# Moving the scan's second copies to ScalarE and the modulations' weight splits to VectorE, in a hybrid diffusion trunk

## The chip, the cores and the metric

The kernel runs on one core of a Trainium2 chip. In this kernel TensorE multiplies matrices, VectorE and ScalarE do most of the elementwise work and fetch the results of matmuls from PSUM, GpSimd does elementwise work between tiles in SBUF, and SyncE issues the transfers. Each engine has a queue of its own. The metric is the device time of one execution in microseconds; lower is better. The median of three runs is what a change is compared with, and the profile is of one execution more.

## The reference: what is computed

One inference step of a two-layer trunk over 128 context tokens and 512 latent tokens, with 1024 channels. Each layer is a normalisation, a modulation by shift, scale and gate, one input projection for three mixers, the mixers, and an output projection:

```
shift, scale, gate = split(silu(cond) @ w_mod[l] + b_mod[l], 3)
h = rmsnorm(x, norm_w[l]) * (1 + scale) + shift
a, b, c, gates = split(h @ w_in[l])
y = sigmoid(ga) * (attention_a(a) @ w_oa) + sigmoid(gb) * (attention_b(b) @ w_ob) + sigmoid(gc) * (scan_c(c) @ w_oc)
x = x + gate * (y @ w_out)
```

The third mixer is a scan over tokens, forward and backward, for 8 heads with a state of 64 x 64 each:

```
sa = state @ a_t
state = state * w_t + outer(sa, b_t) + outer(v_t, k_t)
y_t = state @ r_t
```

## The kernel before

**Numbers in two parts.** The weights come as float32. For every projection the kernel makes two tiles of each weight tile: `whi`, a rounded copy (ScalarE, line 176), and `wlo`, the rest (a subtraction, line 177), and the product is three matmuls instead of one (lines 227 to 229 for the projections). `load_split` does this for two halves of each 128-column block in the stage in question: transfer, cast, subtraction. Which engine subtracts is the argument `sub`: VectorE in most places, GpSimd for the weights inside attention and, before the change, for the modulations' weights.

**The modulations.** `modulation` computes 128 values of shift, scale or gate for both kinds of tokens: it loads and splits a block of `w_mod`, makes 16 matmuls of 4 columns (lines 249 and 250), copies a row and turns it by one more matmul. Layer 0 runs its 8 gate blocks and all 16 shift and scale blocks of layer 1 in this way between other work, layer 1 its own 8 gate blocks. That is 32 calls of two pieces each. They are called from `fillers` and, at the end, from `period`.

**The scan.** It is cut into chunks of 64 tokens: two for the context, eight for the latent tokens, in both directions at once, for four pairs of heads and two layers, which makes 80 steps. `c_scan` does a step as a chain through several engines:

- line 771: matmuls with the keys and the state give `sca` in PSUM;
- lines 773 and 774: two copies of 64 x 128 values bring it to `Wb` in SBUF, one for each head of the pair. Both read the same PSUM bank, and the framework lets the second engine read it only after the first one has ended;
- line 777: matmuls of `Wb` with the inverse matrices give `scb`;
- lines 779 and 780: two such copies bring it to `VZ`, again from one bank;
- line 782: GpSimd copies it to `Ub`; line 786: matmuls for the next state; line 790: matmuls that add to `sca`;
- lines 801 and 803: VectorE makes the next state, which line 771 of the next step reads; line 808: ScalarE copies the output.

**What runs beside it.** While the scan of one pair goes on, `pump` plays a stream of other work between its steps: input projections, gates, the modulations, and the preparation of the next pair. The last is `c_prep`, `c_pairs` and `c_inverse`. The inverse is a loop of 30 steps of two small VectorE instructions each (lines 662 and 664), between a transposition at line 656 and one at line 674, after which TensorE goes on with matmuls of 32 x 32 at line 683. There are eight of these inverses, four in each layer; the first of each layer runs before a scan.

**The order.** The program's order gives the dependences. The framework's scheduler then lays out each engine's queue with its own estimate of durations (`schedule_with_timeline_sim=True`, line 1624), so that instructions of the stream stand between those of one step. Weight tiles have two buffers of each kind (`NW = 2`), and the raw weights two.

Of the kernel before, what the change touches and what calls it, by code (L numbers as in the profile page):

```python
# [107 lines left out]
class Trunk:  # L108
# [595 lines left out]
    def c_scan(self, l, e, ps, rate, prev):  # L704

        nc, V, S, G, PE = self.nc, self.V, self.S, self.G, self.PE
        sm = cs = self.cs
        p, L1, AB, BT, gm, VZ = e.p, e.L1, e.AB, e.BK, e.gm, e.VZ

        def pc(name):  # L710
            return ps.tile([128, 512], F32, tag="c", name=name)

        PR = (slice(0, 64), slice(64, 128))
        QR = (slice(64, 128), slice(0, 64))

        e.YY = YY = cs.tile([128, 20, 64], F32, tag="YY", name="YY")
        step = 0
        for n, base in ((2, 0), (8, 2)):
            ctxp = n == 2
            if ctxp:  # L720
                for h in range(2):
                    G.memset(VZ[h][PR[h], 0:2, :], 0.0)
                Zg = sm.tile([128, 2, 64], F32, tag="Zg", name="Zg", bufs=2)
                G.memset(Zg, 0.0)
            else:
                Z0 = sm.tile([128, 2, 64], F32, tag="Z0", name="Z0")
                nc.sync.dma_start(out=Z0, in_=self.I["zinit"][l, p])
                for h in range(2):
                    r_ = PR[h]
                    S.copy(out=VZ[h][r_, base, :], in_=Z0[r_, 0])  # L730
                    S.mul(out=VZ[h][r_, base + n - 1, :], in_=Z0[r_, 1], mul=gm[r_, 10 + base + n - 1:10 + base + n])

            def pair(cf, cb):

                a, b = base + cf, base + cb
                if a < b:
                    return slice(a, b + 1, b - a)
                return slice(a, b - 1 if b else None, b - a)

            for k in range(n):  # L740
                cf, cb = k, n - 1 - k
                up = pair(cf, cb)
                uu = (base + cf, 10 + base + cb)
                cc = (base + cf, base + cb)
                last = k == n - 1
                need_z = ctxp or not last
                gi = (base + k, None if last else 10 + base + n - 2 - k)
                if need_z and not (ctxp and k == 0):
                    Zg = sm.tile([128, 2, 64], F32, tag="Zg", name="Zg", bufs=2)
                    for h in range(2):  # L750
                        r_ = PR[h]
                        if not last:
                            g2 = gm[r_, gi[0]:gi[1] + 1:gi[1] - gi[0]]
                            G.tensor_tensor(out=Zg[r_], in0=VZ[h][r_, up, :], in1=g2.unsqueeze(2).to_broadcast([64, 2, 64]),
                                            op=ALU.mult)
                        else:
                            G.tensor_scalar(out=Zg[r_, 0], in0=VZ[h][r_, cc[0], :], scalar1=gm[r_, gi[0]:gi[0] + 1],
                                            scalar2=None, op0=ALU.mult)
                            G.tensor_copy(out=Zg[r_, 1], in_=VZ[h][r_, cc[1], :])
                Wb, Ub = self.wbd[step % 2], self.ubd[step % 2]  # L760
                step += 1
                if step == 5 and prev:
                    self.c_out(prev, ps)
                ca, cb_ = pc("sca"), pc("scb")

                a4 = ca[:, 0:256].rearrange("p (d h i) -> p d h i", d=2, h=2)
                b4 = cb_.rearrange("p (x d h i) -> p x d h i", x=2, d=2, h=2)

                for h in range(2):
                    for d in range(2):  # L770
                        PE.matmul(a4[:, d, h], lhsT=L1[h][:, uu[d]].rearrange("p a s -> p (a s)"), rhs=VZ[h][:, cc[d], :],  # L771
                                  start=(h == 0 and d == 0), stop=False, skip_group_check=True)
                S.copy(out=Wb[PR[0], :, 0], in_=a4[0:64, :, 0])
                V.tensor_copy(out=Wb[PR[1], :, 1], in_=a4[0:64, :, 1])
                self.pump(rate)
                for d in range(2):
                    PE.matmul(cb_[:, d * 128:d * 128 + 128], lhsT=AB[:, uu[d]].rearrange("p a s -> p (a s)"),
                              rhs=Wb[:, d].rearrange("p h i -> p (h i)"), start=True, stop=True, skip_group_check=True)
                S.copy(out=VZ[0][PR[0], up, :], in_=b4[0:64, 0, :, 0])  # L779
                V.tensor_copy(out=VZ[1][PR[1], up, :], in_=b4[0:64, 0, :, 1])  # L780
                for h in range(2):
                    G.tensor_copy(out=Ub[PR[h], :, h], in_=VZ[h][PR[h], up, :])  # L782
                self.pump(rate)
                if need_z:
                    for d in range(2):
                        PE.matmul(cb_[:, 256 + d * 128:384 + d * 128], lhsT=BT[:, uu[d]].rearrange("p h i -> p (h i)"),  # L786
                                  rhs=e.VZt[:, :, cc[d], :], start=True, stop=True, skip_group_check=True)
                self.pump(rate)
                for d in range(2):
                    PE.matmul(ca[:, d * 128:d * 128 + 128], lhsT=AB[:, uu[d]].rearrange("p a s -> p (a s)"),  # L790
                              rhs=Ub[:, d].rearrange("p h i -> p (h i)"), start=False, stop=True, skip_group_check=True)
                if need_z:
                    if last:
                        Zf = sm.tile([128, 2, 64], F32, tag="Zf", name="Zf")
                    for h in range(2):
                        r_ = PR[h]
                        for d in range(2):
                            src = b4[r_, 1, d, h]
                            dst = Zf[r_, d] if last else VZ[h][r_, cc[d] + (1 if d == 0 else -1), :]
                            if gi[d] is None:  # L800
                                V.tensor_tensor(out=dst, in0=src, in1=Zg[r_, d], op=ALU.add)
                            else:
                                V.scalar_tensor_tensor(out=dst, in0=src, scalar=gm[r_, gi[d]:gi[d] + 1], in1=Zg[r_, d],  # L803
                                                       op0=ALU.mult, op1=ALU.add)
                    if last:
                        nc.sync.dma_start(out=self.O["nst"][l, p], in_=Zf)
                for h in range(2):
                    S.copy(out=YY[QR[h], uu[0]:uu[1] + 1:uu[1] - uu[0], :], in_=a4[64:128, :, h])
# [547 lines left out]
    def run(self):  # L1356
# [26 lines left out]
        def pool(ctx, name, bufs, **k):  # L1383
            return ctx.enter_context(tc.tile_pool(name=name, bufs=bufs, reuse_waits="tile", **k))

        self.early = set()
        ps = P("psA0", **PSA)
        with ExitStack() as ctx:
            wp = pool(ctx, "wp0", 1, side="right")
# [19 lines left out]
        for l in range(DEPTH):  # L1409
            plan = self.plan = NS(**PLAN[l])  # L1410
            if l:
                ps = P(f"psA{l}", **PSA)
            with ExitStack() as ctx, ExitStack() as ctx_c, ExitStack() as ctx_e:
                wp = pool(ctx, f"wp1{l}", 1)
# [14 lines left out]
                mods = [(l, ct) for ct in range(2 * KT, 3 * KT)]  # L1429
# [4 lines left out]
                def fillers(n):  # L1434
                    for _ in range(n):
                        yield from units.pop(0)
                        count[0] += 1
                        while mods and count[0] >= every:
                            count[0] -= every
                            yield from self.modulation(*mods.pop(0), wp, ps, self.G)  # L1440

                def keys(p):

# [54 lines left out]
                ps = P(f"psB{l}", f=1, pt=2, po=1, S=2)  # L1498
# [3 lines left out]
            ps = P(f"psC{l}", f=8)  # L1502
            with ExitStack() as ctx:
                wp = pool(ctx, f"wp3{l}", 1)
# [137 lines left out]
```

## Time and profile before

| | |
|---|---|
| median of three runs | 2282.05 us (2279.15 to 2290.32) |
| the profiled execution | 2288.99 us |
| its span, first to last instruction | 2287.3 us |
| TensorE busy | 2112.1 us (92%), 15380 matmuls |
| VectorE busy | 1547.8 us (68%), 3096 instructions |
| ScalarE busy | 1155.0 us (50%), 2574 instructions |
| GpSimd busy | 528.7 us (23%), 680 instructions |
| mean granted clock of TensorE | 0.947 of full speed |

The profile lists for each group of instructions the line, the engine, the operation, what it writes and reads, the count, the busy time with the mean of one in ns, and the idle time of the engine just before them with what ended it. PE is TensorE, DVE VectorE, ACT ScalarE, POOL GpSimd, SP SyncE. A wait is put down to the instruction whose semaphore came last.

### The profile page before, as it was taken

How to read it: one execution, taken by the hardware profiler on the slowest of the kernel's cores; microseconds unless marked ns; L12 is line 12 of the kernel's file. 1: busy time of each engine (PE TensorE's matmuls, PEld its weight loads, DVE VectorE, ACT ScalarE, POOL GpSimd, SP SyncE). 2: the span in 40 equal slices, each digit the busy share in tenths (PEclk: the TensorE clock that was granted, in tenths of full speed). 3: DMA queues.
4: the chain of work that ended last, by engine and by line, in shares of the span. 5: the costliest groups of instructions: out<-in, count | busy, mean ns of one | idle time of the engine just before them, and what ended most of it. 6: DMA issues, size and time to landing. Idle time of an engine off the chain costs nothing.

```text
span 2287.3 us, 40446 instructions
## 1 busy us (share of the span) xinstructions
PE 2112.1 (92%) x15380; PEld 2004.8 (88%) x15380; DVE 1547.8 (68%) x3096; ACT 1155.0 (50%) x2574; POOL 528.7 (23%) x680
## 2 busy tenths in 40 slices
PE   8989999999889889999989999998997888899998
PEld 6989999999788768889989999998997876788998
DVE  4666776877845677766647867668576467777673
ACT  4544545554444567762355545545353456677332
POOL 3121324234232221102031022221222222111111
PEclk9998989989899999999999999898897889999999
DMA  6232223222223311036612322232122221111562
GB/s 231 79 96 74 85 78 101 70 89 92 91 87 110 106 38 39 31 101 209 192 53 89 98 75 79 77 101 71 54 94 79 83 88 44 35 47 44 181 194 83
DMA packets 111763, 209.71 MB, mean 92 GB/s; under 512 B 14416, under 2 KB 33488, under 8 KB 111568
## 3 DMA queue, kind: packets, MB, share of 16 engines
q1 hardware_dynamic: 111568, 207.12, 28.3%
q8 instruction: 121, 1.98, 0.4%
q14 instruction: 74, 0.61, 0.1%
HBM read 163.52 MB, written 43.55 MB: 91 GB/s over the span
## 4 chain that ended last, share of the span: by engine, by line
PE 69%; DVE 15%; ACT 8%; issue 4%; DMA 3%; POOL 1%; DVEq 0%; SPq 0%; ACTq 0%; POOLq 0%
PE pcm L227 11%; PE pcm L228 10%; PE pcm L229 10%; PE sc L958 3%; PE pA L612 3%; PE sca L771 2%; PE pm L180 2%; PE pm L182 2%; PE pm L181 2%; PE pp L976 2%; PE scb L786 2%; DVE wlo L177 1%; PE pout L180 1%; PE pout L182 1%; PE pout L181 1%
## 5 line engine op out<-in xcount | busy, mean ns | idle before, releaser
L227 PE MATMUL pcm<-hh,whi 128*128 128x320 f32 x1952 | 630.9, 323 | 21.4 <-DVE modc L254 5.8
L229 PE MATMUL pcm<-hh,wlo 128*128 128x320 f32 x1952 | 621.4, 319 | 7.1 <-DVE wlo L177 7.1
L228 PE MATMUL pcm<-hl,whi 128*128 128x320 f32 x1952 | 620.8, 318 | 0.0
L227 PEld LDWEIGHTS pcm<-hh,whi 128*128 128x128 f32 x1952 | 377.3, 193 | 29.3 <-DVE modc L254 6.8
L229 PEld LDWEIGHTS pcm<-hh,wlo 128*128 128x128 f32 x1952 | 376.3, 193 | 10.4 <-DVE wlo L177 9.4
L228 PEld LDWEIGHTS pcm<-hl,whi 128*128 128x128 f32 x1952 | 377.4, 193 | 1.3
L176 ACT CAST whi<-wraw 128x512 fp32r<-128x512 f32 (+1 forms) x356 | 226.3, 666 | 295.8 <-PE pcm L228 104.1
L177 DVE TENSOR_TENSOR wlo<-wraw,whi 128x512 fp32r<-128x512 f32 (+1 forms) x262 | 208.1, 809 | 84.9 <-ACT whi L176 83.5
L177 POOL TENSOR_TENSOR wlo<-wraw,whi 128x512 fp32r<-128x512 f32 x94 | 123.4, 1328 | 161.4 <-ACT whi L176 126.2
L782 POOL COPY ubd<-VZ 64x128 f32<-64x128 f32 x160 | 62.4, 390 | 406.2 <-ACT VZ L779 345.1
L961 DVE TENSOR_REDUCE nm<-sc 128x1 f32<-128x640 f32 x128 | 104.4, 819 | 27.7 <-PE sc L958 26.3
L166 DVE TENSOR_TENSOR pl<-pp,ph 128x512 fp32r<-128x512 f32 x160 | 107.0, 684 | 22.5 <-ACT ph L165 19.6
L182 PE MATMUL pm<-yh,wlo 128*128 128x320 f32 x384 | 118.9, 310 | 0.3 <-DVE wlo L177 0.3
L180 PE MATMUL pm<-yh,whi 128*128 128x320 f32 x384 | 118.8, 309 | 0.0
L181 PE MATMUL pm<-yl,whi 128*128 128x320 f32 x384 | 118.6, 309 | 0.0
L963 ACT ACTIVATE P<-sc,nm 128x640 f32<-128x640 f32 x128 | 102.0, 798 | 26.7 <-DVE nm L961 22.0
L165 ACT CAST ph<-pp 128x512 fp32r<-128x512 f32 x160 | 91.7, 588 | 37.8 <-PE pp L976 20.3
L976 PE MATMUL pp<-small,P 128*128 128x128 f32 x640 | 98.4, 278 | 2.7 <-ACT RB L1004 2.2
L771 PE MATMUL sca<-VZ,L 128*128 128x64 f32 x640 | 94.6, 286 | 3.0 <-DVE VZ L803 2.2
L771 PEld LDWEIGHTS sca<-VZ,L 128*128 128x128 f32 x640 | 91.2, 208 | 6.0 <-DVE VZ L803 4.0
L976 PEld LDWEIGHTS pp<-small,P 128*128 128x128 f32 x640 | 78.1, 143 | 12.8 <-ACT RB L1004 4.3
L662 DVE TENSOR_TENSOR NF<-LN 128x30 f32<-128x30 f32 (+14 forms) x240 | 84.9, 354 | 6.5
(376 smaller groups left out, 4800.1 us busy)
## 6 DMA issues: line engine op xcount, KB each, us to landing
wraw<-in_win SPq DMA_DIRECT2D x156, 256.0 KB, 3.0
wraw<-in_wg SPq DMA_DIRECT2D x96, 256.0 KB, 3.1
wraw<-in_wmod SPq DMA_DIRECT2D x64, 256.0 KB, 3.0
gsp<-gt SPq DMA_DIRECT2D x48, 320.0 KB, 2.5
gt<-gsp SPq DMA_DIRECT2D x48, 320.0 KB, 3.3
wraw<-in_wo SPq DMA_DIRECT2D x24, 512.0 KB, 4.3
cm<-gsl SPq DMA_DIRECT2D x26, 320.0 KB, 2.6
wraw<-in_wmod SPq DMA_DIRECT2D x16, 512.0 KB, 6.8
```

What stands on the lines that cost most here:

```text
L166: self.V.tensor_tensor(out=lo, in0=src, in1=f32(hi), op=ALU.subtract)
L176: self.S.copy(out=hi[part], in_=raw)
L177: sub.tensor_tensor(out=lo[part], in0=raw, in1=f32(hi[part]), op=ALU.subtract)
L180: self.PE.matmul(out, lhsT=lh, rhs=rh, start=first, stop=False)
L181: self.PE.matmul(out, lhsT=lh, rhs=rl, start=False, stop=False)
L182: self.PE.matmul(out, lhsT=ll, rhs=rh, start=False, stop=last)
L227: PE.matmul(p[0:m, 0:H], lhsT=wh[:, kt], rhs=self.hh[:, kt, rs], start=(kt == 0), stop=False)
L228: PE.matmul(p[0:m, 0:H], lhsT=wh[:, kt], rhs=self.hl[:, kt, rs], start=False, stop=False)
L229: PE.matmul(p[0:m, 0:H], lhsT=wl[:, kt], rhs=self.hh[:, kt, rs], start=False, stop=(kt == KT - 1))
L771: PE.matmul(a4[:, d, h], lhsT=L1[h][:, uu[d]].rearrange("p a s -> p (a s)"), rhs=VZ[h][:, cc[d], :], start=(h == 0 and d == 0), stop=False ...
L961: V.tensor_reduce(out=nm, in_=sc[:, :, 0:H], axis=AX.XY, op=ALU.max, negate=True)
L976: PE.transpose(p[:, qt * 128:(qt + 1) * 128], Ps[qt][:, t * 128:(t + 1) * 128], self.ident)
```

## The change

Two of the four copies in a scan step go from VectorE to ScalarE, which then does all four. The weights of the modulations that `fillers` calls are split by VectorE instead of GpSimd; the call in `period` (line 1477), for what is left of the list then, stays on GpSimd.

```diff
@@ c_scan
                 S.copy(out=Wb[PR[0], :, 0], in_=a4[0:64, :, 0])
-                V.tensor_copy(out=Wb[PR[1], :, 1], in_=a4[0:64, :, 1])
+                S.copy(out=Wb[PR[1], :, 1], in_=a4[0:64, :, 1])
                 self.pump(rate)
...
                 S.copy(out=VZ[0][PR[0], up, :], in_=b4[0:64, 0, :, 0])
-                V.tensor_copy(out=VZ[1][PR[1], up, :], in_=b4[0:64, 0, :, 1])
+                S.copy(out=VZ[1][PR[1], up, :], in_=b4[0:64, 0, :, 1])
                 for h in range(2):
                     G.tensor_copy(out=Ub[PR[h], :, h], in_=VZ[h][PR[h], up, :])
@@ run, fillers
                         while mods and count[0] >= every:
                             count[0] -= every
-                            yield from self.modulation(*mods.pop(0), wp, ps, self.G)
+                            yield from self.modulation(*mods.pop(0), wp, ps, self.V)
```

## Rows read from the trace of the kernel before

**Rows 1.** Busy time by stretch: start:end us, length, engines' busy us (instructions), PEclk, DMA share, GB/s.

```profile
100.00:720.00 620.00, 577.66 (x4558) 559.26 (x4557) 433.20 (x931) 297.39 (x688) 180.50 (x258) 0.92 0.28 88
...
1225.00:1840.00 615.00, 569.15 (x4421) 555.70 (x4420) 424.93 (x927) 289.76 (x667) 141.02 (x232) 0.92 0.25 82
```

**Rows 2.** TensorE's waits, 100 to 720 us: who, ended by, us, times, longest.

```profile
PE scb L777 <- DVE wbd L774: 8.8, 9, 1.4
...
PE scb L786 <- DVE VZ L780: 4.3, 5, 1.3
PE px L683 <- DVE NF L674: 3.6, 2, 3.2
```

**Rows 3.** TensorE's waits, 1225 to 1840 us.

```profile
PE px L683 <- DVE NF L674: 16.1, 2, 9.8
PE scb L777 <- DVE wbd L774: 7.8, 6, 2.6
PE scb L786 <- DVE VZ L780: 5.8, 7, 2.2
```

**Rows 4.** Busy time of two inverses, engines in the order PE, PEld, DVE, ACT, POOL.

```profile
1559.80:1604.50 44.70, 31.92 (x214) 30.74 (x212) 41.01 (x104) 20.99 (x54) 8.27 (x14) 0.81 0.26 79
1699.50:1742.00 42.50, 33.69 (x244) 32.79 (x243) 38.38 (x98) 19.06 (x51) 4.81 (x14) 0.95 0.34 112
```

**Rows 5.** Groups by shape: count, busy us, mean ns, idle before, ended by.

```profile
L177 DVE TENSOR_TENSOR wlo<-wraw,whi 128x512 fp32r<-128x512 f32 x222 | 152.8, 706 | 73.5 <-ACT whi L176 72.1
L177 POOL TENSOR_TENSOR wlo<-wraw,whi 128x512 fp32r<-128x512 f32 x94 | 123.4, 1328 | 161.4 <-ACT whi L176 126.2 <-DVE bonus L573 24.4 <-PE pcm L228 6.0
...
L774 DVE COPY wbd<-sca 64x128 f32<-64x128 f32 x80 | 22.7, 284 | 39.3 <-ACT wbd L773 37.5
```

**Rows 6.** VectorE's waits for ScalarE's copies, whole span.

```profile
DVE VZ L780 <- ACT VZ L779: 44.0, 27, 4.4
...
DVE wbd L774 <- ACT wbd L773: 37.5, 24, 3.5
```

**Rows 7.** Timeline at 1587 us: start us, length us, instruction, idle before.

```profile
1586.92 0.26 ACT L773 COPY wbd<-sca 64x128 f32<-64x128 f32 x1
...
1589.13 0.28 DVE L774 COPY wbd<-sca 64x128 f32<-64x128 f32 x1
...
1589.47 0.58 PE L777 MATMUL scb<-wbd,AB 128*128 128x128 f32 x1 [2.59 <-DVE wbd L774]
```

**Rows 8.** Timeline at 1765 us, a step with nothing beside it.

```profile
1764.88 0.26 ACT L773 COPY wbd<-sca 64x128 f32<-64x128 f32 x1 [0.62 <-PE sca L771]
1765.17 0.28 DVE L774 COPY wbd<-sca 64x128 f32<-64x128 f32 x1 [0.89 <-ACT wbd L773]
...
1765.51 0.71 PE L777 MATMUL scb<-wbd,AB 128*128 128x128 f32 x4 [0.72 <-DVE wbd L774]
```

**Rows 9.** Timeline at 447 us, VectorE's inverse and GpSimd's splits.

```profile
447.48 2.73 POOL L177 TENSOR_TENSOR wlo<-wraw,whi 128x512 fp32r<-128x512 f32 x2
447.71 1.36 DVE L664 TENSOR_TENSOR LN<-LN,NF 128x220 f32<-128x220 f32 x1
449.10 1.36 DVE L662 TENSOR_TENSOR NF<-LN 128x228 f32<-128x228 f32 x1
450.50 0.40 DVE L664 TENSOR_TENSOR LN<-LN,NF 128x228 f32<-128x228 f32 x1
```

**Rows 10.** Busy time and granted clock around the end of two inverses, as rows 1.

```profile
1310.00:1345.00 35.00, 33.69 (x327) 32.99 (x327) 15.66 (x34) 11.43 (x28) 5.67 (x11) 0.85 0.17 55
1590.00:1625.00 35.00, 25.04 (x246) 24.38 (x245) 22.81 (x52) 12.97 (x33) 8.61 (x15) 0.54 0.08 28
```

**Rows 11.** Timeline of TensorE at 218 us.

```profile
218.29 0.78 PE L771 MATMUL sca<-VZ,L 128*128 128x64 f32 x6
218.91 0.72 PE L489 MATMUL pk<-small,rb 128*128 128x128 f32 x5
219.46 0.33 PE L771 MATMUL sca<-VZ,L 128*128 128x64 f32 x2
```

## The prediction

> **What bounds the kernel now.** I read the busy time by stretch first, for the two stretches in which a scan runs, 100 to 720 us and 1225 to 1840 us [rows 1]. TensorE is busy for 577.66 of 620 us and 569.15 of 615 us there; VectorE for about 70% of the time, ScalarE for 48%, GpSimd for 29% and 23%. So TensorE sets the end, and what an edit can give is bounded by TensorE's idle time in the two stretches: 42.3 + 45.9 = 88.2 us, and by what its clock (0.92 granted on the mean) adds to that. Then the list of waits, TensorE's alone, in each stretch [rows 2, 3]: the longest entries are ended by VectorE. Line 777 waits for the second scan copy (8.8 + 7.8 = 16.6 us, 15 times), line 786 for the second copy of the other pair (4.3 + 5.8 = 10.1 us, 12 times), line 683 for the last transposition of the inverse (3.6 + 16.1 = 19.7 us, 4 times). The change touches all three. Last I read the stretch of an inverse, from the transposition of line 656 to that of line 674: VectorE is busy for 41.01 of 44.7 us and for 38.38 of 42.5 us there [rows 4]. In these stretches (eight, about 45 us each) VectorE is the bound, and line 683 pays where TensorE has nothing left in front of it.
>
> **The copies.** The change takes 160 copies of 284 ns from VectorE [rows 5], 45.4 us, and gives them to ScalarE, whose first copy of the same shape takes 0.26 us [rows 7, 8]: 41.6 us. Now the second copy waits for the first one to end, since both read one PSUM bank, and it does so at the head of VectorE's queue: VectorE stood idle 37.5 us before line 774 and 44.0 us before line 780 [rows 6], with weight splits, state updates and the inverse's steps queued behind it. On ScalarE the second copy follows the first with no handover.
>
> What TensorE gets of that is read at each of its 15 waits at line 777. They are of two kinds. In eight, VectorE comes late. The largest [rows 7]: ScalarE's copy ends at 1587.18, VectorE's begins at 1589.13, behind two weight splits, and TensorE idles 2.59 us. With the second copy 0.27 us behind the first, it would have its tile 1589.41 - 1587.18 - 0.27 = 1.96 us earlier. In the other seven, the scan's own chain is late [rows 8]: VectorE starts 0.03 us after ScalarE's end, and the gain is 0.31 - 0.27, about 0.05 us of a wait of 0.72 us. Summed in this way, the smaller of the wait and of that lead at each place, line 777 gives 8.7 of 16.6 us. The 12 waits at line 786 give 4.8 of 10.1 us (five late ones 4.1, seven of about 0.1). Ends: 0, if TensorE only finds its next wait, and 26.7 us, if all of both go.
>
> The copies also leave the inverse. Where line 683 stalls for long, at 321, 1604 and 1742 us, 6, 7 and 6 of them lie inside the VectorE stretch in front of it, by the timeline: 19 x 0.284 = 5.4 us off the 19.7 us. Ends: 0 and 19.7 us.
>
> ScalarE has 41.6 us more to do. Its other work moves back by up to 0.27 us per copy: the casts of line 176, the copies of line 808, the tanh of the gates. The cover is that it idles for half of both stretches. All the idle time of TensorE that the three rows above don't explain is 88.2 - 46.4 = 41.8 us, and it goes with 587 us of ScalarE's busy time at most; in proportion, 41.6 us more cost 41.8 x 41.6 / 587 = 3.0 us. Ends: 0 and 41.6 us. I take 3.0.
>
> **The splits.** Of the 32 modulations 31 come from `fillers` (23 of layer 0's 24: the running sum of line 1437 ends a rounding short of the last, which line 1477 then runs on GpSimd as before). In two pieces that is 62 splits from GpSimd (1328 ns) to VectorE (706 ns) [rows 5]: GpSimd loses 82.3 us, VectorE gains 43.8 us, about what the copies took. In the lists that rows 2 and 3 are taken from, TensorE waits for no split of GpSimd, so a faster split alone gives nothing. On VectorE each stands in an in-order queue and waits there for its cast: the 222 that are there now waited 72.1 us for ScalarE, 0.33 us each, so 62 make 20 us, against the 81.5 us of waiting that the copies leave. Queued behind such a wait are the state updates of line 803 and the inverse's 60 steps, and TensorE's lines 771 and 683 wait for those. One modulation on VectorE is 2 x (0.706 + 0.33) = 2.1 us. Layer 0 runs 23 of them in some 650 us, 1.6 in the 45 us of an inverse, 3.3 us against 1.7 us of copies removed; layer 1 has 8, a third of that.
>
> What covers the difference is a stall that goes. While GpSimd runs two splits from 447.48 to 450.21, two steps of the inverse take 1.36 us each, and the step after them, of the same size as the second, 0.40 us [rows 9]. So a pair of splits on GpSimd costs VectorE 1.9 us where it meets such steps, and that goes with the pair. The Trainium skill has a rule that cuts the other way too ("SBUF — State Buffer", section "Who interferes with whom"): a VectorE instruction with two SBUF inputs and a GpSimd instruction that reads SBUF exclude each other, whichever came first, for the whole instruction. By it the 62 moved splits, which have two SBUF inputs, would now hold up GpSimd's copies of line 782 and so TensorE at line 790; by the row the move gives 1.9 us per pair, by the rule it may give them back there, which is the first rival's time.
>
> I take 0 for the splits: 3.3 - 1.7 - 1.9 us per inverse in layer 0, nothing or less in layer 1. Ends: -4 us (two pairs fall out of inverses, 2 us each) and +10 us (1.6 us in each of the six inverses that run beside a scan, if no stall goes).
>
> **The clock.** Around the end of an inverse with no stall the granted clock was 0.85 over 35 us; around that of the one that stalled for 9.85 us, 0.54 [rows 10]. These are means over the two levels, 2.4 and 1.2 GHz; before the second, TensorE had idled. The difference is 0.31 x 35 = 10.9 us of work at full speed. The stalls shrink and don't vanish, so I take 3 us back, ends 0 and 10.9.
>
> **Sum.** -8.7 - 4.8 - 5.4 + 3.0 + 0 - 3 = -18.9 us on the profiled execution's own 2288.99 us (span 2287.3, the rest around it 1.7): 2270.1. That execution lies 6.9 us over the median of the three runs shown, 2282.05, so I forecast 2282.05 - 18.9 = 2263 us.
>
> **The rivals.**
> First, the gain goes to the next wait: TensorE arrives early at line 777 and waits longer at 786, 790 or 771, since a scan step is a chain of copies. For it: in the seven waits of the second kind nothing but the chain is late [rows 8]. Against it: in the other eight, projection matmuls stand ready behind the scan's. It leaves the inverse's 5.4 us less ScalarE's 3.0: 2280. The same time comes out if ScalarE has a cast of 0.6 us between the two copies, so that the change doesn't do what it says.
>
> Second, more than forecast: the 81.5 us that VectorE waited at the head of its queue [rows 6] let the inverse end early, and the stalls at 1604 and 1742 us go with their clock. A further 14 us of line 683 and 8 us of clock: 2241.
>
> Third, slower: VectorE becomes the bound in more inverses. The price of a modulation there is 2.1 us, the copies pay 1.7; it decides from one modulation per inverse on, if GpSimd's splits were not in the way before (they fell into four of eight). Two inverses that now have no stall then go the way of the one at 1604 us, each with the 10.9 us of clock and some 4 us of stall: +30, less the 13.5 of the copies: +16, 2298. For it: VectorE is above 90% there [rows 4]; against it: the three longest stalls had no split of GpSimd in their inverse, nor one to be put there if the order stays.
>
> Fourth, the order is laid out anew. TensorE's order isn't the program's: five matmuls of line 489 stand between the sixth and the seventh of line 771 [rows 11], which one loop issues without a break. So the build orders by its own estimate of durations, and other engines mean other places. The same code has stalls of 0 to 9.85 us at line 683 in eight inverses; a new draw of these is worth 10 us either way, here taken as the worse side: 2275.
>
> **How the numbers follow.** Chances: the forecast and what lies near it 0.42, the second rival 0.10, the first 0.18, the third 0.18, the fourth's worse side 0.12. The range leaves out the far half of the second and of the third, 0.14 in all: 2240 to 2297. About 0.5% (11.4 us) is what a measurement of this kernel can tell from no change. Faster by more than that, under 2270.6: 0.42 + 0.10 = 0.52. Within it: the first, the fourth and a part of the third, 0.32. Slower, over 2293.5: 0.16.
>
> **What would show it.** Right: the wait at line 777 ended by ScalarE and at or under 8 us in all, line 786 at or under 6; ScalarE busy near 1195 us, GpSimd near 446, VectorE unchanged within 25 us (1548 less the time of steps like those of rows 9); no inverse step of 1.3 us beside a split of GpSimd in the scans; line 683 near 14 us. Wrong: line 683 over 25 us in all, or TensorE's waits for casts (line 229 behind line 177) grown by more than 5 us, or the granted clock of the two stretches under 0.91.

## The result, and the profile after

The kernel is faster with the change: 2246.97 us median of four runs (2241.23 to 2256.08) against 2281.77 us for the kernel before in the same comparison. The ratio is 0.9845 [0.9802, 0.9887], that is 34.8 us less. The forecast was 2263 us with a range of 2240 to 2297: the sign and the range held, but the gain is 1.8 times the 18.9 us that were worked out. The profiled execution of after took 2248.71 us, its span 2246.9 us, which is 40.4 us under the span of before (2287.3 us). Of the experiments below, one execution of e7 (2353.04 us) and one of e8 (4030.27 us) lay far above the others of their kernel and are left out of medians and ratios; the latter is the one that was profiled, so no row of e8 is read.

The page of after: span, busy time of the engines, and TensorE's granted clock in tenths over 40 slices.

```profile
span 2246.9 us, 40407 instructions
PE 2095.5 (93%) x15380; PEld 1993.5 (89%) x15380; DVE 1519.9 (68%) x2998; ACT 1200.9 (53%) x2734; POOL 448.1 (20%) x618
...
PEclk9998999999799899999999999899896999999999
```

ScalarE has 45.9 us more than before, of which the moved copies are 41.2, and GpSimd has 80.6 us less, near the 82.3 us that the moved splits took there. The groups by shape of after, which answer to [rows 5], show the moved work itself.

```profile
L177 DVE TENSOR_TENSOR wlo<-wraw,whi 128x512 fp32r<-128x512 f32 x284 | 194.2, 704 | 108.8 <-ACT whi L176 103.8 <-PE pmod L253 3.6
...
L177 POOL TENSOR_TENSOR wlo<-wraw,whi 128x512 fp32r<-128x512 f32 x32 | 40.7, 1289 | 60.0 <-ACT whi L176 59.9
...
L774 ACT COPY wbd<-sca 64x128 f32<-64x128 f32 x80 | 20.6, 258 | 1.1
L780 ACT COPY VZ<-scb 64x128 f32<-64x128 f32 x80 | 20.6, 258 | 1.9
```

The second copies take 258 ns each and ScalarE is idle for 1.1 and 1.9 us in all before 160 of them: they follow the first copy at once. 62 splits have moved, 222 to 284 on VectorE and 94 to 32 on GpSimd.

TensorE's waits in after, whole span: who waits, ended by what, us in total, times, longest us. They answer to [rows 2, 3].

```profile
PE px L683 <- DVE NF L674: 14.7, 3, 12.7
...
PE scb L777 <- ACT wbd L774: 7.5, 11, 1.3
PE scb L786 <- ACT VZ L780: 6.3, 10, 0.7
...
PE px L683 <- DVE mean L823: 4.1, 1, 4.1
...
PE pcm L229 <- DVE wlo L177: 3.5, 3, 2.4
```

Line 777 went from 16.5 us over the span to 7.5, line 786 from 10.1 to 6.3, and the longest wait at either is now 1.3 us, so the late copies are gone and the waits that the scan's chain makes are left. Line 683 hardly moved: 19.8 us before, 14.7 + 4.1 = 18.8 us after.

Two entries carry the difference of the two spans. TensorE's idle time is the span less its busy time: 175.2 us before, 151.4 after, 23.8 less. Its busy time is for the same 15380 matmuls: 2112.1 us before, 2095.5 after, 16.6 less. Together 40.4 us, which is the whole difference. Most of the second entry is the clock. TensorE was at 1.2 GHz for 242.1 us of the span before and for 208.8 after. An estimate of what that cost: the busy time of the matmuls that ran at 1.2 GHz, less what as many of the same line and shape took on the mean at 2.4 GHz in the traces of before, after and nine of the experiments, is 84.8 us before and 74.3 after, 10.5 less. That is 0.35 of the time at 1.2 GHz and not half of it; TensorE was idle for 40.6 and 38.2 us of that time, and the matmuls of line 683 took about as long at either level. The whole difference lies in the two scans, from the first matmul of line 771 to the last copy of line 808 of a layer. Before (rows as in [rows 1]):

```profile
113.80:724.80 611.00, 568.65 (x4495) 550.48 (x4494) 421.54 (x915) 288.16 (x669) 179.95 (x255) 0.92 0.27 87
1266.00:1831.80 565.80, 525.19 (x4106) 513.06 (x4104) 390.01 (x875) 259.58 (x604) 132.86 (x223) 0.91 0.25 81
```

After, the same two stretches, with the same number of TensorE's instructions within seven:

```profile
113.50:704.90 591.40, 554.65 (x4496) 539.63 (x4494) 408.33 (x875) 310.37 (x748) 126.58 (x215) 0.94 0.28 90
1250.00:1794.10 544.10, 523.04 (x4113) 513.02 (x4112) 373.47 (x809) 284.04 (x688) 118.46 (x213) 0.92 0.26 85
```

The scans take 41.3 us less in all (1176.8 to 1135.5); what lies outside them takes 0.9 us more in all, 3.9 more between the scans and 2.7 less behind the second.

### The profile page after: what moved, and what is told of

Same layout as the page of the kernel before. It is cut to its first block, busy times and chain, and to the rows that moved or that the text cites. A ratio compares the mean times of both kernels' runs of the same rounds, so it can differ in the third digit from the quotient of the medians.

```text
span 2246.9 us, 40407 instructions
## 1 busy us (share of the span) xinstructions
PE 2095.5 (93%) x15380; PEld 1993.5 (89%) x15380; DVE 1519.9 (68%) x2998; ACT 1200.9 (53%) x2734; POOL 448.1 (20%) x618
## 4 chain that ended last, share of the span: by engine, by line
PE 73%; DVE 11%; ACT 8%; issue 3%; DMA 3%; POOL 1%; SPq 0%; DVEq 0%; ACTq 0%; POOLq 0%
PE pcm L227 11%; PE pcm L228 11%; PE pcm L229 11%; PE pA L612 3%; PE sc L958 3%; PE sca L771 3%; PE pm L180 2%; PE pm L182 2%; PE pm L181 2%; PE pp L976 2%; PE scb L786 2%; PE scb L777 2%; PE sca L790 2%; PE pout L180 1%; PE pout L182 1%
## 5 line engine op out<-in xcount | busy, mean ns | idle before, releaser
L176 ACT CAST whi<-wraw 128x512 fp32r<-128x512 f32 (+1 forms) x356 | 226.1, 666 | 274.8 <-PE pcm L228 109.7
L177 DVE TENSOR_TENSOR wlo<-wraw,whi 128x512 fp32r<-128x512 f32 (+1 forms) x324 | 248.6, 785 | 119.1 <-ACT whi L176 113.8
L963 ACT ACTIVATE P<-sc,nm 128x640 f32<-128x640 f32 x128 | 102.1, 799 | 25.7 <-DVE nm L961 20.8
L803 DVE SCALAR_TENSOR_TENSOR VZ<-scb,gm,Zg 64x64 f32<-64x64 f32 x256 | 62.2, 280 | 40.6 <-PE scb L786 33.6
L976 PEld LDWEIGHTS pp<-small,P 128*128 128x128 f32 x640 | 78.0, 143 | 12.8 <-ACT RB L1004 4.3
L612 PE MATMUL pA<-L,BK 128*128 128x128 f32 x640 | 85.5, 276 | 4.0 <-ACT AB L617 3.7
```

The source lines that it names most:

```text
L176: self.S.copy(out=hi[part], in_=raw)
L177: sub.tensor_tensor(out=lo[part], in0=raw, in1=f32(hi[part]), op=ALU.subtract)
L612: PE.matmul(pA[:, j * 128:(j + 1) * 128], lhsT=BK[:, u].rearrange("p a s -> p (a s)"), rhs=L1[h][:, u].rearrange("p a s -> p (a s)"), star ...
L976: PE.transpose(p[:, qt * 128:(qt + 1) * 128], Ps[qt][:, t * 128:(t + 1) * 128], self.ident)
```

## The experiments

The theories that the expectations weigh are, in words: that TensorE gains what it waited for the late second copies (the first); that GpSimd's splits, which stretch the inverse on VectorE, are a good part; that a new order of the build is what one sees; and, formed after the first runs, that VectorE's standing at the head of its queue behind ScalarE's copy is the main cost (the fourth). Each kernel ran 4 to 12 times, beside 11 to 17 runs of before, whose median in the three comparisons was 2284.55 us (e1 to e4), 2283.65 (e5 to e8) and 2285.34 (e9 to e12). "Half of the time at 1.2 GHz" is the mean over a kernel's runs of the span times one less the granted clock; for before it is 116.5 us, with a scatter of 6.7 us from run to run. It says how long the clock was low and is more than that cost: over 42 runs of before the span moved by 0.66 us with each us of it, and by the estimate above it is 0.7. The last column has TensorE's busy and idle time in the profiled execution, which add up to its span; in before they are 2112.1 and 175.2 us.

| kernel | median us | ratio to before | half of the time at 1.2 GHz | TensorE busy, idle us |
|---|---|---|---|---|
| the change | 2246.97 | 0.9845 [0.9802, 0.9887] | 99.4 | 2095.5, 151.4 |
| e1, both copies, no splits | 2250.23 | 0.9848 [0.9827, 0.9869] | 90.0 | 2095.7, 155.3 |
| e2, splits alone | 2273.82 | 0.9951 [0.9934, 0.9969] | 119.3 | 2105.2, 169.4 |
| e3, copy of line 774 alone | 2255.47 | 0.9872 [0.9853, 0.9890] | 94.7 | 2095.6, 158.9 |
| e4, all four copies on VectorE | 2279.73 | 0.9983 [0.9964, 1.0001] | 112.0 | 2114.5, 170.1 |
| e5, copy of line 780 alone | 2247.18 | 0.9829 [0.9810, 0.9847] | 90.9 | 2086.3, 152.6 |
| e6, before, more stream per slot | 2270.25 | 0.9942 [0.9919, 0.9964] | 109.7 | 2103.6, 164.9 |
| e7, the change, as e6 | 2234.96 | 0.9788 [0.9763, 0.9814] | 95.7 | 2090.9, 144.4 |
| e8, the change, no split on GpSimd | 2260.61 | 0.9884 [0.9864, 0.9904] | 101.1 | not read |
| e9, e1 with a wait put back on VectorE | 2258.05 | 0.9885 [0.9853, 0.9917] | 94.4 | 2095.2, 161.0 |
| e10, e9's copies without the wait | 2251.98 | 0.9848 [0.9814, 0.9882] | 92.7 | 2098.8, 151.4 |
| e11, e5 with e6's rates | 2249.38 | 0.9849 [0.9815, 0.9883] | 94.4 | 2092.5, 153.7 |
| e12, the change, still more per slot | 2238.98 | 0.9794 [0.9757, 0.9832] | 99.5 | 2097.4, 141.6 |

The ten kernels that have a second copy on ScalarE lie at 0.9788 to 0.9885 of before and the three others (e2, e4, e6) at 0.9942 to 0.9983, though the build lays out the queues of each by itself. So where the second copies stand carries the gain, and not one lucky order.

### e1: the copies alone

```diff
-                V.tensor_copy(out=Wb[PR[1], :, 1], in_=a4[0:64, :, 1])
+                S.copy(out=Wb[PR[1], :, 1], in_=a4[0:64, :, 1])
...
-                V.tensor_copy(out=VZ[1][PR[1], up, :], in_=b4[0:64, 0, :, 1])
+                S.copy(out=VZ[1][PR[1], up, :], in_=b4[0:64, 0, :, 1])
```

> The two copies on ScalarE alone; the modulations' splits stay on GpSimd. First theory (the copies' waits at lines 777 and 786 and what they leave in VectorE's queue carry the gain): 0.985 to 0.990 of before, so at least two thirds of the 34.8 us; TensorE's waits at line 777 near 8 us and at 786 near 6 us; VectorE about 45 us less busy than before; inverse steps of 1.3 us beside GpSimd's splits are still there. Second theory (the splits' stall of VectorE was the larger part): 0.993 to 0.998. Third theory (a new order of the queues gives and takes by chance): any value, and one that doesn't add up with the run of the splits alone.

Measured: 0.9848, the whole gain of the change and just past the first theory's range. TensorE's waits:

```profile
PE px L683 <- DVE NF L674: 15.4, 5, 8.3
...
PE pcm L229 <- DVE wlo L177: 7.2, 8, 2.6
PE scb L777 <- ACT wbd L774: 6.8, 10, 1.3
PE scb L786 <- ACT VZ L780: 6.2, 9, 0.9
```

Lines 777 and 786 are where they are in after, and TensorE's busy time (2095.7 us) fell as far. Line 664 of the inverse in the same run (shortest, median, longest ns of 240) still has its long steps:

```profile
L664 DVE TENSOR_TENSOR LN<-LN,NF x240: 180/351/1449, 152.1 to 1702.3; 128x30 f32<-128x30 f32 x8, 128x84 f32<-128x84 f32 x8, 128x130 f32<-128x130 f32 x8, 128x168 f32<-128x168 f32 x8
```

The kernel with these steps is as fast as the one without them.

### e2: the splits alone

```diff
-                            yield from self.modulation(*mods.pop(0), wp, ps, self.G)
+                            yield from self.modulation(*mods.pop(0), wp, ps, self.V)
```

> The modulations' splits on VectorE alone; the copies stay where they were. First theory: no gain, 0.998 to 1.006, since VectorE has 43.8 us more and keeps waiting about 80 us for ScalarE's copies at the head of its queue; line 777 waits at least the 16.5 us of before. Second theory: 0.985 to 0.992, as no inverse step is stretched to 1.3 us any more. Third theory: any value.

Measured: 0.9951, between what the theories expected; line 777 waits 13.7 us, where the first theory wanted at least 16.5. TensorE's waits:

```profile
PE px L683 <- DVE NF L674: 21.7, 5, 7.7
...
PE scb L777 <- DVE wbd L774: 13.7, 14, 2.8
PE scb L786 <- DVE VZ L780: 10.6, 13, 1.8
...
PE px L683 <- DVE mean L823: 6.2, 1, 6.2
```

The long steps of the inverse are gone; line 664 of this run:

```profile
L664 DVE TENSOR_TENSOR LN<-LN,NF x240: 184/350/568, 149.8 to 1722.6; 128x30 f32<-128x30 f32 x8, 128x84 f32<-128x84 f32 x8, 128x130 f32<-128x130 f32 x8, 128x168 f32<-128x168 f32 x8
```

So GpSimd's splits do stretch the inverse, and without them line 664 has no step over 568 ns; but line 683 waits 27.9 us here, more than before. What the splits give alone is half a per cent, and next to the copies nothing that can be told (0.9845 and 0.9848). Half a per cent is also what e6 shows for a shift of the order, so it isn't settled whether the splits themselves give it.

### e3 and e5: one copy each

e3:

```diff
-                V.tensor_copy(out=Wb[PR[1], :, 1], in_=a4[0:64, :, 1])
+                S.copy(out=Wb[PR[1], :, 1], in_=a4[0:64, :, 1])
```

> Only the copy of line 774 on ScalarE, the copy of line 780 and the splits as before. First theory: about half of the run with both copies, 0.990 to 0.995; the wait at line 777 falls from 16.5 to about 8 us, the one at 786 stays near 10 us. Second theory: 0.997 to 1.0.

e5:

```diff
-                V.tensor_copy(out=VZ[1][PR[1], up, :], in_=b4[0:64, 0, :, 1])
+                S.copy(out=VZ[1][PR[1], up, :], in_=b4[0:64, 0, :, 1])
```

> Only the copy of line 780 on ScalarE; the copy of line 774 stays on VectorE, the splits on GpSimd. If the two copies' gains add up, the run with line 774 alone (0.9872) and the one with both (0.9848) leave 0.2% for this one: 0.996 to 0.999. If the gain comes from any one of the two leaving VectorE's queue, and the second adds little, 0.985 to 0.990. By the lateness read at the waits of before (4.8 us at line 786 against 8.7 us at 777): 0.993 to 0.996.

Measured: 0.9872 and 0.9829, both faster than any of the ranges expected. TensorE's waits in e3:

```profile
PE px L683 <- DVE mean L823: 12.7, 2, 6.8
...
PE scb L786 <- DVE VZ L780: 11.3, 15, 2.0
PE scb L777 <- ACT wbd L774: 7.8, 11, 1.3
```

and in e5:

```profile
PE scb L777 <- DVE wbd L774: 8.7, 10, 1.4
...
PE px L683 <- DVE NF L674: 7.2, 4, 5.8
PE scb L786 <- ACT VZ L780: 6.7, 12, 0.7
PE px L683 <- DVE mean L823: 5.9, 1, 5.9
```

The waits went as the first theory says at the line whose copy moved: 7.8 us at line 777 in e3 while line 786 stayed at 11.3; 6.7 us at line 786 in e5. In e5 line 777 fell to 8.7 us as well, though its second copy is still on VectorE. The times did not follow these two waits: either copy alone gives most or all of the 1.5%, and the two don't add up. The last column of the table says where that is: against before, TensorE's busy time is 16.5 us less in e3 and 25.8 in e5, with both copies 16.4, and its idle time 16.3 and 22.6 us less, with both 19.9. (e5's profiled execution is its fastest one, 6.6 us under its median.)

### e4: all four copies on VectorE

```diff
-                S.copy(out=Wb[PR[0], :, 0], in_=a4[0:64, :, 0])
+                V.tensor_copy(out=Wb[PR[0], :, 0], in_=a4[0:64, :, 0])
...
-                S.copy(out=VZ[0][PR[0], up, :], in_=b4[0:64, 0, :, 0])
+                V.tensor_copy(out=VZ[0][PR[0], up, :], in_=b4[0:64, 0, :, 0])
```

> All four copies of a step on VectorE, the splits as before: no handover between the two copies of a pair, but VectorE has 45 us more and ScalarE 41 us less. If the handover and VectorE's idle wait for ScalarE's copy were the cost, this is as fast as the run with both copies on ScalarE. If it is how late VectorE comes to a copy (first theory), it is slower than before, 1.005 to 1.02, and line 777 waits more than 16.5 us.

Measured: 0.9983, no change, and 13.6 us at line 777, where a slower kernel and over 16.5 us were expected: a miss. TensorE's waits, and below them two of the copies in the groups by shape:

```profile
PE scb L777 <- DVE wbd L774: 13.6, 14, 2.3
...
PE scb L786 <- DVE VZ L780: 12.1, 13, 2.0
```

```profile
L774 DVE COPY wbd<-sca 64x128 f32<-64x128 f32 x80 | 22.7, 284 | 1.2
L773 DVE COPY wbd<-sca 64x128 f32<-64x128 f32 x80 | 22.5, 281 | 28.1 <-PE sca L771 26.8
```

Here both copies of a bank stand on one engine and the second follows the first (1.2 us of idle before 80 of them), so the handover from ScalarE to VectorE is gone. TensorE's two waits are 25.7 us all the same, against 26.6 before. Waits of this size thus need no handover. What before and e4 share is that the second copy stands in VectorE's queue, behind other work, as [rows 7] show for the largest wait. Whether in e4 a handover saved and the load added cancel each other, this run alone doesn't tell. The 160 copies more on VectorE, with which its busy time rose from 1547.8 to 1585.4 us, cost nothing that can be measured, which speaks against any account in which VectorE's load is the bound.

### e6, e7, e11 and e12: another order

The rates say how much of the stream `pump` plays in a slot of the scan, one for each layer. e6 changes them in the kernel before, e7 in the changed kernel, e11 in e5's; e12 takes 1.05 and 0.85 in the changed kernel.

```diff
-    dict(share=[7, 5, 5, 7, 13], fb=[0, 0, 3], at=[3, 2, 1, 0, 2, 1], rate=1.0,
+    dict(share=[7, 5, 5, 7, 13], fb=[0, 0, 3], at=[3, 2, 1, 0, 2, 1], rate=1.02,
...
-    dict(share=[8, 6, 7, 7, 9], fb=[0, 0, 1], at=[3, 0, 2, 0, 2, 0], rate=0.8,
+    dict(share=[8, 6, 7, 7, 9], fb=[0, 0, 1], at=[3, 0, 2, 0, 2, 0], rate=0.82,
```

> The kernel before with the stream played a little faster beside the scan (rate 1.02 and 0.82 for 1.0 and 0.8): no work is changed, only the order of the queues. If the order alone moves the time by as much as the change did (third theory), it lands more than 0.7% off, either way. If the engine of the copies is what counts, 0.996 to 1.004.

> The changed kernel with the same rates (1.02 and 0.82). If the engine of the copies is what counts, 0.980 to 0.989 of before, whatever the order. If the changed kernel's order was a lucky one, over 0.991.

> Only the copy of line 780 on ScalarE, with the rates 1.02 and 0.82. If the engine's effect (0.9829) and that of the rates (0.9942 on the kernel before) multiply, 0.975 to 0.980. If what one gives the other can't give again, 0.981 to 0.985.

> The changed kernel with the rates 1.05 and 0.85. If a faster stream shortens the last stretch of each scan further, 0.972 to 0.979 of before; if 1.02 and 0.82 were only another order, anywhere from 0.978 to 0.990.

Measured: 0.9942, 0.9788, 0.9849 and 0.9794. e6 lies between its two ranges and e7 just under its lower one; e11 came out as it was to be if one gain leaves less for the other, e12 just past the end of its first range and within the second. e7 over e6 is 0.9788 / 0.9942 = 0.9845, the ratio of the change itself: its gain holds at these rates too. e6 is no pure reordering: in its profile the scans are 2.6 us shorter and what lies outside them 16 us, since part of the stream that ran after a scan now runs in it. The two steps add up for the change (e7) but not for e5 (e11 is no faster than e5). e7 is the fastest kernel measured, by the medians 2.1% under before and 0.5% under after; e12 is level with it.

### e8: no split on GpSimd at all

```diff
-            self.sub = self.G
+            self.sub = self.V
...
-                        yield from self.modulation(*m, wp, ps, self.G)
+                        yield from self.modulation(*m, wp, ps, self.V)
```

> The changed kernel, and GpSimd splits no weights at all: those of attention and of the last modulation go to VectorE too. If VectorE's load doesn't bound the kernel outside the scans either, a little faster than the changed kernel, as the steps that GpSimd's splits stretch there (5.8 us of VectorE in all) go: 0.981 to 0.985 of before. If attention's chain waits for VectorE, which is busy for 68% of it, slower than the changed kernel: 0.986 to 0.992.

Measured: 0.9884, within the second range, and 0.4% slower than the change by the ratios, at the edge of what the intervals tell apart. Moving the last 32 splits off GpSimd gives nothing.

### e9 and e10: VectorE's wait, put back by itself

To e1, e9 adds two copies of one column per scan step on VectorE, which read what ScalarE's second copies have just written and write a tile that nobody reads. VectorE so waits again for ScalarE at those two places, and TensorE doesn't. In e10 the same copies read a constant.

```diff
+                V.tensor_copy(out=self.junk[PR[1], 0:1], in_=Wb[PR[1], 0, 1, 0:1])
...
+                V.tensor_copy(out=self.junk[PR[1], 1:2], in_=VZ[1][PR[1], cc[0], 0:1])
```

> Both copies on ScalarE as in the first run, and behind each of them VectorE copies one column of what ScalarE has just written into a tile that nobody reads: VectorE waits again for ScalarE at the head of its queue, twice a step, and TensorE waits for none of it. This repeats part of no needed work; the results are the same. If VectorE's wait at the head of its queue was the cost (fourth theory), most of the gain goes: 0.993 to 1.0 of before. If it was TensorE's own wait for a late second copy (first theory), the gain stays, less a little for 160 small instructions: 0.984 to 0.989.

> The same 160 small copies on VectorE, reading a constant: they wait for nothing. Both theories: 0.984 to 0.989 of before. What the run before this one is over this one is the price of the waits alone.

Measured: 0.9885 and 0.9848, both in the first theory's range, medians 6.1 us apart, with intervals that overlap. VectorE's waits in e9 show that the wait is there (line numbers are shifted by two or three):

```profile
DVE junk L783 <- ACT VZ L782: 42.1, 31, 4.8
DVE junk L776 <- ACT wbd L775: 37.2, 31, 3.8
```

These 79.3 us are the 81.5 us of [rows 6] over again. By the means of the runs they cost 8.4 us (2259.0 against 2250.7), which the scatter leaves at 3 to 13, and TensorE's idle time is 9.6 us longer in e9. The fourth theory falls as the main cost: VectorE's standing idle is a tenth to two fifths of what the copies won back, and not most of it.

## Why the prediction was right or wrong

**What bounds the kernel.** Right. TensorE is at 93%, the whole gain is in its idle time and its busy time, most of the latter the clock, and it lies in the two scans.

**Lines 777 and 786.** Right in size, and in mechanism as far as the runs go. Predicted 8.7 + 4.8 = 13.5 us; measured 9.0 + 3.8 = 12.8 us. The split of the waits into late copies and the chain's own [rows 7, 8] gave it; by the timeline seven of the waits at line 777 are of the late kind and eight of the other, not eight and seven, which leaves the sum at 8.7. e1 and e3 show that it is the copies, [rows 7] and e4 that a copy is late by its place in VectorE's queue and that no handover is needed for it. But in e5 line 777 falls by 7.8 us although its own copy did not move, so it isn't shown that all of the 9.0 us come from that copy and none from the new order of the queues.

**The inverse.** The step "19 x 0.284 = 5.4 us off the 19.7 us" failed: line 683 gave 1.0 us. It took the copies out of the stretches and supposed that nothing comes in their place. The trace says that something does. From the first step of line 662 or 664 to the last, summed over the eight inverses:

| | length us | their own steps | VectorE's other work in between |
|---|---|---|---|
| before | 281.8 | 169.0 | 108.1 |
| after | 284.3 | 160.3 | 127.2 |
| e1 | 283.9 | 167.5 | 119.6 |

The inverses are no shorter. Without the copies the build puts more of VectorE's other work between their steps; with the splits on VectorE still more of it, while the steps themselves lose 8.7 us. Rival four, the new order, is what line 683 shows: the stall of 9.8 us in layer 1 went to 1.6, and one of 12.7 us came in the fourth inverse of layer 0.

**The splits.** Taken at 0. Next to the copies that holds within what can be measured; alone they give 0.5% (e2). The 1.9 us per pair that the prediction charged to GpSimd is about right: five pairs fell into the inverses of before, the steps lost 8.7 us, and in after none takes over 593 ns, where e1 has 1449. By the Trainium skill ("SBUF — State Buffer", section "Who interferes with whom") the moved splits could hold up GpSimd's copies of line 782 in turn; here their mean went from 390 to 395 ns, and TensorE's wait at line 790, 4.0 us in before, is no longer among its waits in after, so what the rule might give back isn't seen.

**ScalarE's load.** About right. TensorE's idle time that ScalarE ended rose from 53.1 to 68.6 us, of which 7.5 + 6.3 = 13.8 us are the copies', which VectorE ended before; so its other work costs 1.7 us more, where 3.0 were taken. What this row lacks is the other side: the waits at lines 229 (7.1 to 3.5 us) and 790 (4.0 to nothing), and line 227 behind line 254 (5.8 to 2.0 us), together 11.4 us, which the prediction left at 0. In e1 the first of these is still 7.2 and the last 4.6 us, and the second is gone: some 6 of the 11.4 us go with the splits, and the 4.0 of line 790 with the copies.

**The clock.** This is the term that was mis-sized: 3 us were taken, with 10.9 as the upper end, and by the estimate above it is 10.5 us in the profiled executions; with the copies alone it is 18.0 (84.8 to 66.8). (Half of the time at 1.2 GHz fell by 17.1 us as the mean of the runs, and by 26.5 in e1. But with the 19.9 us of idle time 26.5 is more than the 36.3 us by which e1's span is shorter, so the half is too much.) The other 6.1 of the 16.6 us by which TensorE's busy time fell are at the full clock and have no term in the sum; no run shows what they are. The step that failed is the reading of [rows 10], which put the low clock down to the stall at line 683. Its 0.31 x 35 us is too much as work, too, since TensorE was idle for 10 of these 35 us. Two windows of before, around the end of an inverse with a stall of 0.42 us, say otherwise:

```profile
470.00:505.00 35.00, 34.42 (x325) 33.42 (x324) 21.30 (x45) 17.27 (x43) 11.57 (x21) 0.76 0.16 53
...
478.00:495.00 17.00, 17.00 (x194) 16.75 (x192) 12.50 (x27) 7.58 (x19) 6.86 (x6) 0.51 0.20 64
```

From 478 to 495 us TensorE is busy the whole time, nearly all of it at 1.2 GHz. Until 486 us it has the 80 matmuls of line 683 and the 80 of line 695, each of 32 x 32 values with 32 columns, which end every inverse; the other 9 us are larger matmuls. In before the clock fell during line 683's matmuls at five of the eight ends, with or without a stall, and at three before them, in or behind waits; how long it stays low differs. Line 683's small matmuls pay next to nothing for it, 4.01 us at 2.4 GHz and 4.10 at 1.2 GHz, and line 695's 1.5 us each time, 2.41 and 3.91. At 2.4 GHz, in after:

```profile
1296.94 4.01 PE L683 MATMUL px<-NF,AB 32*32 32x32 f32 x80
...
1305.79 2.41 PE L695 MATMUL py<-AB,LN 32*32 32x32 f32 x80
```

At 1.2 GHz, in before:

```profile
616.88 4.10 PE L683 MATMUL px<-NF,AB 32*32 32x32 f32 x80
...
621.53 3.91 PE L695 MATMUL py<-AB,LN 32*32 32x32 f32 x80
```

The rest is paid by the larger matmuls at the low level: in before a matmul of the projections starts 0.15 us after the one ahead of it at 474 us, and 0.27 us after it at 493. Most of what changes between the kernels is at these eight places. Time at 1.2 GHz, from 12 us before line 683's matmuls to 40 us after them, over the eight, and in all:

| | before | after | e1 | e2 | e3 | e4 | e5 | e6 |
|---|---|---|---|---|---|---|---|---|
| at the eight ends, us | 162.5 | 136.5 | 119.5 | 157.1 | 112.6 | 168.7 | 95.6 | 140.7 |
| whole span, us | 242.1 | 208.8 | 188.3 | 233.5 | 191.2 | 253.0 | 171.4 | 215.7 |
| what it cost, estimate as above, us | 84.8 | 74.3 | 66.8 | 80.2 | 66.8 | 88.9 | 60.0 | 76.2 |

Of the 33.3 us by which after is lower over the span 26.0 lie there, of e1's 53.8 us 43.0. The kernels with a second copy on ScalarE and the splits on GpSimd (e1, e3, e5) are lowest, at 95.6 to 119.5 us; those with both second copies on VectorE (before, e2, e4, e6) lie at 140.7 to 168.7, and e6 shows that the rates, too, move it by 22. The third inverse of layer 1 shows how. Around its end e1 has this window, and in TensorE's groups of that window this row:

```profile
1565.00:1600.00 35.00, 35.00 (x331) 34.74 (x331) 23.64 (x50) 16.16 (x34) 7.81 (x11) 0.80 0.25 82
```

```profile
L227 PE MATMUL pcm<-hh,whi 128*128 128x320 f32 x40 | 13.3, 332 | 0.0
```

Before has 0.54 there, in the second window of [rows 10], and in the groups of that window:

```profile
L683 PE MATMUL px<-NF,AB 32*32 32x32 f32 x80 | 4.1, 231 | 9.8 <-DVE NF L674 9.8
...
L227 PE MATMUL pcm<-hh,whi 128*128 128x320 f32 x9 | 3.9, 430 | 0.0
```

In e1 TensorE has 40 matmuls of line 227 (and about as many of lines 228 and 229) to do around the small ones, in before 9, and a stall. I read from this that the projection work left over when an inverse ends goes with both, the stall and the time that the clock stays low; the stall and the low clock themselves also leave room for fewer matmuls in 35 us, so the count alone doesn't say which comes first. After itself has such a place too, at its 12.7 us stall (the first row here); the second row is its third inverse of layer 0, which in before had the 0.76 above:

```profile
585.00:620.00 35.00, 20.46 (x218) 19.44 (x219) 16.32 (x41) 9.93 (x24) 5.93 (x14) 0.56 0.13 43
...
450.00:485.00 35.00, 35.00 (x350) 34.51 (x349) 15.43 (x30) 14.58 (x33) 6.10 (x13) 0.90 0.24 80
```

Shown are the places where the time at 1.2 GHz changes and how much of it there is; its price is an estimate. That it is the projection work left over is argued from these windows; no run changed that alone. Why moving either one of the two copies is enough to bring the clock back stays open, as does why the splits on VectorE take some of it away again (74.3 us in after against 66.8 in e1). TensorE's busy time is the same in these two, 2095.5 and 2095.7 us.

**The rivals.** The first, that the gain goes to the next wait, falls: lines 777 and 786 fell together and line 771's wait didn't grow (2.2 to 1.7 us). The second had the size nearly right (2241 us) and the wrong reason: line 683 didn't give way, and e9 prices VectorE's freed waits at 3 to 13 us, where this rival gave them 22 us over the forecast. The third, that VectorE becomes the bound, falls: e2 puts the splits on it without taking the copies, e4 gives it all four copies, and neither is slower. The fourth (2263 and its 10 us make 2273, not 2275) did happen at line 683, but it doesn't carry the result, since e7 over e6 gives the same ratio and all ten kernels with a moved copy are faster than the three without.

**The signs that were named.** As expected: line 777 ended by ScalarE at 7.5 us (8 or less), ScalarE at 1200.9 us (1195), GpSimd at 448.1 (446), no step of 1.3 us, no growth at line 229, the clock of the two stretches of [rows 1] at 0.94 and 0.92. Just off: line 786 at 6.3 us (6 or less), VectorE 27.9 us under before (25). Off: line 683 at 18.8 us (14).

## What to carry to other kernels

When TensorE waits for the second of two copies out of PSUM, look at what is queued ahead of that copy rather than at the busy share of its engine: moving one or both to a queue where they follow at once gave 1.3 to 1.7% here, while 160 copies more on the busier engine cost nothing that could be measured. Where the build orders the queues by itself, time that an edit frees inside a stretch can be refilled, as in the inverses here, so it is no gain until the wait at the end of the stretch gets shorter. Look for the low clock in all places, also those where the engine is busy, and not at the stalls alone; and price it by what the matmuls there would have taken at the full clock, not by half of the time at the low level. By that estimate it gave 0.4 us for each us of idle time that went with the change, and 0.9 with the copies alone.

## What the runs showed of the hardware that was not expected

- The clock was at 1.2 GHz over nearly all of 17.00 us (0.51 granted) in which TensorE was busy for 17.00 us, beginning in a run of 80 matmuls of 32 x 32 values with a wait of 0.42 us ahead of it.
- 80 matmuls of 32 x 32 values took 4.01 us at 2.4 GHz and 4.10 us at 1.2 GHz at line 683, and 2.41 and 3.91 us at line 695.
- The same program gets a different clock from run to run: over 42 runs of before the granted clock lay between 0.942 and 0.955, and the time followed it with a correlation of -0.85, by 0.66 us of span for each us that half of the time at 1.2 GHz grew.
- A copy of 64 x 128 values from PSUM took 258 ns on ScalarE and 284 ns on VectorE.
